# Mixer weights: the lo part made by a ScalarE copy and an adding transfer instead of a VectorE subtraction

## The chip, the cores and the metric

The kernel runs on one core of one Trainium2 chip. The core has five engines that run side by side, each in the order of its own program: TensorE (PE in the views, PEld for its weight loads), VectorE (DVE), ScalarE (ACT), GpSimd (POOL) and SyncE (SP), which here issues the DMA transfers. They wait for one another through semaphores. The metric is device time in microseconds (us), lower is better.

## What is computed

Two transformer networks, one after the other, on one sequence of 512 tokens with 1024 features, all in float32. Cut to its stages:

```python
def first_block(x, ...):
    for layer in range(2):
        h = rmsnorm(x, norm_mix[layer])
        x = x + (even_mixer(h, ...) if layer == 0 else odd_mixer(h, ...))
        x = x + square(relu(rmsnorm(x, norm_mlp[layer]) @ w_up[layer])) @ w_down[layer]
    return rmsnorm(x, norm_final)

def second_block(x, ...):
    h = x + hybrid_mixer(rms_norm(x, attn_norm_g), ...)
    u = rms_norm(h, ffn_norm_g)
    h = h + (silu(u @ w_gate) * (u @ w_up)) @ w_down
    return rms_norm(h, final_norm_g)
```

The even mixer projects to queries, keys and values of two kinds of attention with eight heads each (one with a forget gate, one in chunks with a relative bias) and projects the joined heads back. The odd mixer has stick-breaking attention and an attention with latent queries and keys. The hybrid mixer has differential attention, and attention over compressed, selected and windowed keys, gated and merged. So a mixer is a set of matrix products with weights around many small softmax chains; an MLP is matrix products with weights alone.

## The kernel before, in words

Activations lie with features on the 128 partitions and the 512 tokens along the free side. Every matrix product with weights is made of three passes in a fast reduced float32 form: a value is split into a hi part (rounded to that form) and a lo part (the rest), and the product is hi x hi + hi x lo + lo x hi. Weights are packed in DRAM in blocks of 128 partitions by at most 1120 columns, mostly 1024 (512 KB, eight tiles of 128 x 128). Method `wblock` (L585) fetches and splits one block: SyncE loads it into a buffer `wr` (two of these), ScalarE copies it into `wh`, the hi part, with rounding, and VectorE writes `wl`, the lo part, as `wr - wh`. `wh` and `wl` have two buffers each. `gemm` (L595) and `gemm_iter` then issue for each of the eight tiles two matmuls with `wh` and one with `wl`, 24 of 512 columns for a block; `gemm_tok` (L614) uses the block as the moving side, with the lo part in the second matmul of a group. All matmuls of a group add into one PSUM tile and so keep their order.

All operations are first recorded, with their dependencies, by class `Recorder`; `schedule` then lays them out once, before the launch. It simulates the engines with fixed costs (`cost`, L322) and latencies, gives out buffers in turn, and so fixes the order of each engine's program; a transfer costs its issuer 450 or 625 ns there, and lands 650 ns after the issue and its bytes at 360 per ns, one transfer after another (L477). On the chip that order stays, whatever the real durations. All rows of the trace therefore have one line, L372, that of the issuing helper; operations are told apart by their tiles.

Names that matter beside `wr`, `wh`, `wl`: `h` normalised activations; `psg`, `pss`, `psp`, `pso` PSUM tiles for products, scores, transposes and heads; `AB`, `QS`, `KK` queries and keys, split by ScalarE and VectorE and moved into the heads' layout by SyncE's transfers; `x`, `P` softmax tiles and the residual, parked in DRAM as `xs`; `sm` small columns, sums among them; `acc` sums of squares; `rbcq` and `acc` also hold weights of the compression. In the softmax, VectorE adds the bias and takes the extremum, ScalarE exponentiates, VectorE inverts the sum, GpSimd multiplies by it.

The first two blocks of all, of `fox_v0`, are fetched by `load` between the loads of the eight tiles of x. The names of the weights used below: those that begin with up, down or gate belong to the MLPs, yb and out2 are the last two products of the hybrid mixer, and all others are in the mixers.

Of the kernel before, what the change touches and what calls it, by code (L numbers as in the profile page):

```python
# [11 lines left out]
F32 = mybir.dt.float32  # L12
F32R = mybir.dt.float32r
I32 = mybir.dt.int32
AF = mybir.ActivationFunctionType
ALU = mybir.AluOpType
AX = mybir.AxisListType

T = 512
# [226 lines left out]
def size(ap):  # L246
    return math.prod(n for _, n in ap.ap[1:])


class Recorder:  # L250
# [71 lines left out]
    def cost(self, op):  # L322
        n = max(size(a) for a in op.acc[1] + op.acc[0])
        out = op.args[0]
        psum = any(str(a.space).endswith("PSUM") for a in op.acc[0])
        e = op.eng
        k = sum(isinstance(a, AP) for a in op.args[2:]) + sum(isinstance(a, AP) for a in op.kw.values())
        if op.name == "dma_start":
            return 450 if str(op.args[1].space).endswith("DRAM") else 625
        if e == "tensor":  # L330
            n = size(out)
            if op.name == "transpose":
                return 107
            if op.args[2].dtype == F32:
                return max(4 * n / 2.4, 428)
            return n / 2.4 + 2.5
        if e == "scalar":
            return 93 + 0.833 * n - (40 if psum else 0) + 93 * k
        if e == "vector":
            if op.name == "reciprocal":  # L340
                return 67 + 6.3 * n
            if op.name in ("memset", "tensor_copy") or (op.name == "tensor_scalar" and not psum):
                return 67 + 0.53 * n + 58 * k
            if op.name == "scalar_tensor_tensor":
                return 67 + 1.05 * n + 60 * (k - 1)
            return 67 + 1.05 * n
        if op.name == "tensor_scalar":
            return 160 + 0.836 * n + 83 * k
        if op.name == "affine_select":
            return 90 + 1.2 * n  # L350
        if op.name == "memset":
            return 36 + 0.83 * n
        return 958 if n <= 4 else 60 + 2.3 * n
# [37 lines left out]
    def schedule(self):  # L391
# [25 lines left out]
        dma, last, table = 0.0, None, TABLE[AF.Exp]  # L417
# [4 lines left out]
        while len(order) < len(ops):  # L422
            best = None
            for e in engs:
                if avail[e]:
                    s = clock[e]
                elif pend[e]:
                    s = max(clock[e], pend[e][0][0])
                else:
                    continue  # L430
                if best is None or s < best[0]:
                    best = (s, e)
            if best is None:
                raise RuntimeError("no instruction is ready: " + str({t: len(w) for t, w in waiting.items() if w}))
            now, e = best
            while pend[e] and pend[e][0][0] <= now:
                k = heapq.heappop(pend[e])[1]
                heapq.heappush(avail[e], (ops[k].prio, k))
            op = ops[heapq.heappop(avail[e])[1]]
            need = [t for t in op.tiles if t not in held]  # L440
            short = None
            for t in need:
                tag = self.tag[t]
                if not free[tag] or turn[t] != at[tag]:
                    short = tag
            if short is not None:
                waiting[short].append(op.n)
                continue
            late = max([free[self.tag[t]][0] for t in need], default=0.0)
            if late > now:  # L450
                heapq.heappush(pend[e], (late, op.n))
                continue
            for t in need:
                tag = self.tag[t]
                heapq.heappop(free[tag])
                held.add(t)
                at[tag] += 1
                for k in waiting[tag]:
                    heapq.heappush(pend[ops[k].eng], (now, k))
                waiting[tag] = []  # L460
            cost = op.cost
            if e == "tensor":
                stat = self.region(op.args[1])
                if stat != last:
                    cost = max(cost, 107)
                last = stat
            elif op.name == "activation" and TABLE.get(op.args[2], table) != table:
                table = TABLE[op.args[2]]
                cost += 1280
            end = now + cost  # L470
            clock[e] = end
            lat = self.LAT[e]
            if op.name == "tensor_tensor_reduce":
                lat = dict.fromkeys(lat, 425)
            if op.name == "dma_start":
                nbytes = 4 * math.prod(n for _, n in op.args[0].ap)
                dma = max(dma, end + 650) + nbytes / 360  # L477
                end = dma
            op.end = end
            order.append(op)  # L480
            for k in op.succ:
                o = ops[k]
                o.ready = max(o.ready, end + lat.get(o.eng, 0))
                o.left -= 1
                if not o.left:
                    heapq.heappush(pend[o.eng], (o.ready, o.n))
            for t in op.tiles:
                users[t] -= 1
                done_at[t] = max(done_at.get(t, 0.0), end + 200)
                if not users[t]:  # L490
                    tag = self.tag[t]
                    heapq.heappush(free[tag], done_at[t])
                    for k in waiting[tag]:
                        heapq.heappush(pend[ops[k].eng], (now, k))
                    waiting[tag] = []
# [7 lines left out]
class Net:  # L503
# [36 lines left out]
    def c(self, key):  # L540
        o, n = self.cst_at[key]
        return self.ct[:, o:o + n]

    BUFS = {"x": 8, "T": 3, "G": 3, "P": 3, "wr": 2, "wh": 2, "wl": 2, "V": 8, "o": 6, "KK": 4, "QS": 2, "AB": 2, "h": 8, "X4": 4,
            "sm": 16, "sm32": 3, "rbc": 1, "rbcq": 1, "strip": 2}
    PBUFS = {"g": 3, "s": 2, "p": 2, "o": 1}

    def tl(self, tag, shape, dt=F32):
        self.n += 1
        bufs = self.BUFS.get(tag, 1)  # L550
        return self.rec.own(self.sb.tile(shape, dt, tag=tag, name=f"{tag}_{self.n}", bufs=bufs), tag, bufs)
# [33 lines left out]
    def wblock(self, key, b, tags=("wh", "wl")):  # L585
        nc = self.nc
        off, w = self.pk.index[key][0][b]
        raw = self.tl("wr", [128, WB])[:, :w]
        hi, lo = (self.tl(t, [128, WT if t[0] == "w" else 1024], F32R) for t in tags)
        nc.sync.dma_start(raw, self.ins["w"][off:off + 128 * w].rearrange("(p c) -> p c", p=128))  # L590
        nc.scalar.activation(hi[:, :w], raw, AF.Copy)
        nc.vector.tensor_tensor(lo[:, :w], raw, hi[:, :w].bitcast(F32), ALU.subtract)
        return hi, lo

    def gemm(self, key, mov, evac, tags="gggggggg", cols=slice(0, 512), kept=None):  # L595
# [1152 lines left out]


def build(pk, vec, cst, arrays, stages=None, reorder=True, **tck):  # L1750
    nc = bacc.Bacc("TRN2", target_bir_lowering=False, num_devices=1)
    ins = {k: nc.dram_tensor(f"in_{k}_dram", a.shape, mybir.dt.from_np(a.dtype), kind="ExternalInput").ap()
           for k, a in arrays.items()}
    out = nc.dram_tensor("out_0_dram", (D, T), F32, kind="ExternalOutput").ap()
    with tile.TileContext(nc, **tck) as tc, ExitStack() as ctx:  # L1755
        net = Net(ctx, tc, pk, vec, cst, ins, out)
        net.run(stages)
        net.rec.run(tc, reorder)
    nc.rec = net.rec
    return nc  # L1760
# [7 lines left out]
```

## Time and profile before

| | us |
|---|---|
| median of three runs | 2078.53 (2075.46 to 2080.16) |
| the profiled execution, its own time | 2076.13 |
| its span, from the first to the last instruction | 2074.1 |
| TensorE busy | 2017.1 |
| VectorE busy | 1131.8 |
| ScalarE busy | 895.1 |
| GpSimd busy | 396.5 |

Busy time of an engine is the time in which at least one of its instructions ran; matmuls overlap, so a busy TensorE need not run at its peak. "Idle before" is the time an engine stood still ahead of an instruction, with the engine or transfer whose signal ended it. The stretches used below are the first mixer (0 to 300 us), the first MLP (300 to 600), the second mixer (600 to 925), the second MLP (925 to 1250), and the third mixer (1250 to 1600, its last two products follow); the bounds are rounded.

### The profile page before, as it was taken

The numbers are of one execution on the slowest core, as the hardware profiler recorded it, in microseconds if no ns is written. First come the engines' busy times: TensorE is split into PE (matmuls) and PEld (weight loads), VectorE is DVE, ScalarE is ACT, GpSimd is POOL, SyncE is SP. The second block draws the span as 40 slices with busy tenths as digits, with TensorE's granted clock in tenths as the row PEclk, the third lists the DMA queues.
The fourth block names the chain that finished last, engine by engine and source line by source line (L and its number), as shares of the span: only waits on it lengthen the run. The fifth ranks groups of instructions, "written<-read, shape, count | busy, mean of one in ns | idle before, by whom it ended". The sixth has DMA issues, their size and how long they took to land. (4 is left out here: it accounts for less than half of the span.)

```text
span 2074.1 us, 27228 instructions
## 1 busy us (share of the span) xinstructions
PE 2017.1 (97%) x9958; PEld 1683.7 (81%) x9958; DVE 1131.8 (55%) x2033; ACT 895.1 (43%) x1621; POOL 396.5 (19%) x524
## 2 busy tenths in 40 slices
PE   8999999999999999999999999989999999999998
PEld 7888878888888877778888888867788888888887
DVE  5667853434445576774434344766786644333334
ACT  5556542322335555653323243543685543222224
POOL 2343210000022463220000014211340221011013
PEclk9999999999999999999999999999999999999999
DMA  6445623333344315632333334473213222223232
GB/s 199 129 129 154 198 83 100 94 99 97 97 139 127 102 62 131 180 115 92 102 93 101 94 122 135 122 182 116 71 42 112 92 101 92 101 93 102 91 102 82
DMA packets 80293, 231.98 MB, mean 112 GB/s; under 512 B 11424, under 2 KB 15392, under 8 KB 80160
## 3 DMA queue, kind: packets, MB, share of 16 engines
q1 hardware_dynamic: 80160, 230.25, 36.8%
q8 instruction: 78, 1.28, 0.3%
q14 instruction: 55, 0.45, 0.1%
HBM read 183.04 MB, written 10.49 MB: 93 GB/s over the span
## 5 line engine op out<-in xcount | busy, mean ns | idle before, releaser
L372 PE MATMUL psg<-h,wh 128*128 128x512 f32 x2688 | 848.4, 393 | 0.9 <-ACT h L372 0.6
L372 ACT ACTIVATE wh<-wr 128x1024 fp32r<-128x1024 f32 (+3 forms) x313 | 326.3, 1042 | 846.0 <-PE psg L372 672.9
L372 PEld LDWEIGHTS psg<-h,wh 128*128 128x128 f32 x2688 | 503.3, 189 | 102.0 <-ACT h L372 1.5
L372 PE MATMUL psg<-h,wl 128*128 128x512 f32 x1344 | 528.9, 393 | 1.2 <-DVE wl L372 1.0
L372 DVE TENSOR_TENSOR wl<-wr,wh 128x1024 fp32r<-128x1024 f32 (+3 forms) x313 | 384.7, 1229 | 59.9 <-ACT wh L372 58.7
L372 PEld LDWEIGHTS psg<-h,wl 128*128 128x128 f32 x1344 | 253.6, 189 | 53.9 <-DVE wl L372 3.1
L372 PE MATMUL psg<-KK,wh 128*128 128x512 f32 (+1 forms) x788 | 237.8, 383 | 0.4 <-DVE V L372 0.2
L372 DVE TENSOR_TENSOR x<-psg,x 128x512 f32<-128x512 f32 (+1 forms) x120 | 78.2, 654 | 281.8 <-PE psg L372 281.7
L372 POOL TENSOR_TENSOR acc<-acc,T 128x512 f32<-128x512 f32 (+1 forms) x50 | 72.9, 1457 | 775.7 <-issue 627.3
L372 PE MATMUL psg<-V,wh 128*128 128x512 f32 (+1 forms) x672 | 205.7, 387 | 1.1 <-DVE G L372 1.1
L372 PEld LDWEIGHTS psg<-KK,wh 128*128 128x128 f32 x788 | 146.3, 188 | 29.5 <-ACT o L372 0.6
L372 PE MATMUL psg<-KK,wl 128*128 128x512 f32 (+1 forms) x394 | 150.8, 383 | 0.0
L372 PEld LDWEIGHTS psg<-V,wh 128*128 128x128 f32 x672 | 125.6, 188 | 27.3 <-ACT wh L372 1.2
L372 DVE SCALAR_TENSOR_TENSOR T<-psg,rbc 128x512 f32<-128x512 f32 x64 | 44.2, 691 | 167.2 <-PE psg L372 166.8
L372 ACT ACTIVATE x<-x,sm 128x128 f32<-128x128 f32 (+1 forms) x192 | 106.6, 558 | 54.7 <-DVE sm L372 53.9
L372 PE MATMUL psg<-V,wl 128*128 128x512 f32 (+1 forms) x336 | 129.9, 387 | 0.0
L372 PE MATMUL psg<-o,wh 128*128 128x512 f32 x384 | 126.2, 397 | 0.8 <-ACT wh L372 0.5
L372 PE MATMUL psg<-wh,h 128*128 128x256 f32 (+2 forms) x560 | 114.5, 292 | 6.6 <-ACT wh L372 6.6
L372 PE MATMUL pso<-pt,V 128*128 128x128 f32 (+3 forms) x432 | 108.8, 340 | 3.4 <-ACT pt L372 1.9
L372 POOL TENSOR_SCALAR x<-x,sm 128x128 f32<-128x128 f32 (+1 forms) x112 | 65.9, 594 | 174.6 <-DVE sm L372 122.8
L372 PEld LDWEIGHTS psg<-wh,h 128*128 128x128 f32 x560 | 92.4, 194 | 8.4 <-ACT wh L372 6.6
L372 POOL TENSOR_TENSOR T<-T,rbc 128x512 f32<-128x512 f32 x22 | 39.2, 1782 | 280.5 <-ACT T L372 280.5
(263 smaller groups left out, 2667.6 us busy)
## 6 DMA issues: line engine op xcount, KB each, us to landing
wr<-in_w_dram SPq DMA_DIRECT2D x302, 512.0 KB, 3.5
KK<-AB SPq DMA_DIRECT2D x48, 256.0 KB, 5.4
QS<-AB SPq DMA_DIRECT2D x48, 128.0 KB, 4.0
x<-xs SPq DMA_DIRECT2D x24, 256.0 KB, 3.3
xs<-P SPq DMA_DIRECT2D x16, 256.0 KB, 3.9
xs<-x SPq DMA_DIRECT2D x16, 256.0 KB, 2.0
h<-AB SPq DMA_DIRECT2D x16, 256.0 KB, 4.1
KK<-AB SPq DMA_DIRECT2D x32, 128.0 KB, 2.3
```

The lines of the kernel that those rows point to most:

```text
L372: op.inst = getattr(getattr(nc, op.eng), op.name)(*op.args, **op.kw)
```

## The change

For the weights of the mixers, all but those that begin with up, down, gate, yb or out2, the lo part is made otherwise. ScalarE writes the hi part as before, then, in a second instruction, the negated hi part into the lo buffer. GpSimd then issues a transfer that reads the same block from DRAM once more and adds it to what the lo buffer holds. VectorE has no part in it, and the buffer `wr` is read by ScalarE's first copy alone. `wh` and `wl` get three buffers for all weights. The scratch memory for the descriptors of transfers that GpSimd issues is set to 4096 bytes a partition. The planner counts 860 ns of GpSimd for such an issue and a landing 1500 ns later than for one of SyncE.

```diff
@@ cost
         if op.name == "dma_start":
+            if op.eng == "gpsimd":
+                return 860
             return 450 if str(op.args[1].space).endswith("DRAM") else 625
@@ schedule
                 dma = max(dma, end + 650) + nbytes / 360
-                end = dma
+                end = dma if e == "sync" else dma + 1500
@@ Net
-    BUFS = {"x": 8, "T": 3, "G": 3, "P": 3, "wr": 2, "wh": 2, "wl": 2, "V": 8, "o": 6, "KK": 4, "QS": 2, "AB": 2, "h": 8, "X4": 4,
+    BUFS = {"x": 8, "T": 3, "G": 3, "P": 3, "wr": 2, "wh": 3, "wl": 3, "V": 8, "o": 6, "KK": 4, "QS": 2, "AB": 2, "h": 8, "X4": 4,
@@ wblock
-        nc.sync.dma_start(raw, self.ins["w"][off:off + 128 * w].rearrange("(p c) -> p c", p=128))
-        nc.scalar.activation(hi[:, :w], raw, AF.Copy)
-        nc.vector.tensor_tensor(lo[:, :w], raw, hi[:, :w].bitcast(F32), ALU.subtract)
+        src = self.ins["w"][off:off + 128 * w].rearrange("(p c) -> p c", p=128)
+        nc.sync.dma_start(raw, src)
+        if key.startswith(("up", "down", "gate", "yb", "out2")):
+            nc.scalar.activation(hi[:, :w], raw, AF.Copy)
+            nc.vector.tensor_tensor(lo[:, :w], raw, hi[:, :w].bitcast(F32), ALU.subtract)
+        else:
+            nc.scalar.activation(hi[:, :w], raw, AF.Copy)
+            nc.scalar.activation(lo[:, :w], hi[:, :w].bitcast(F32), AF.Copy, scale=-1.0)
+            nc.gpsimd.dma_start(lo[:, :w], src, accum_op=ALU.add)
@@ build
-    nc = bacc.Bacc("TRN2", target_bir_lowering=False, num_devices=1)
+    nc = bacc.Bacc("TRN2", target_bir_lowering=False, num_devices=1, dynamic_dma_scratch_size=4096)
```

## Rows read from the trace of the kernel before

**Rows 1.** The page, part 1: busy us, share of the span, instructions.
```profile
PE 2017.1 (97%) x9958; PEld 1683.7 (81%) x9958; DVE 1131.8 (55%) x2033; ACT 895.1 (43%) x1621; POOL 396.5 (19%) x524
```

**Rows 2.** Busy us by stretch: length, engines, granted clock, DMA share, GB/s.
```profile
0.00:300.00 300.00, 285.40 (x1576) 243.40 (x1577) 201.28 (x439) 166.43 (x348) 92.70 (x160) 0.99 0.53 151
600.00:925.00 325.00, 305.89 (x1625) 256.84 (x1624) 218.32 (x415) 180.05 (x375) 114.80 (x187) 0.98 0.43 121
1250.00:1600.00 350.00, 337.04 (x1813) 276.39 (x1812) 242.55 (x634) 186.51 (x429) 92.41 (x110) 0.99 0.39 111
300.00:600.00 300.00, 300.00 (x1325) 248.39 (x1325) 125.78 (x141) 94.23 (x117) 5.38 (x3) 1.00 0.33 101
925.00:1250.00 325.00, 325.00 (x1435) 269.11 (x1435) 138.64 (x162) 109.20 (x138) 11.65 (x8) 1.00 0.33 102
```

**Rows 3.** Matmuls by shape (busy us, mean ns): first mixer, second mixer, first MLP.
```profile
L372 PE MATMUL psg<-h,wh 128*128 128x512 f32 x315 | 105.0, 403 | 0.6 <-ACT h L372 0.6
...
L372 PE MATMUL psg<-h,wh 128*128 128x512 f32 x265 | 85.9, 398 | 0.0
...
L372 PE MATMUL psg<-h,wh 128*128 128x512 f32 x422 | 129.9, 389 | 0.0
```

**Rows 4.** TensorE's waits, whole span: waiter, releaser, us in total, times, longest.
```profile
PE psg L372 <- ACT wh L372: 7.1, 2, 6.6
PE psg L372 <- DMA rbcq<-in_w_dram: 5.5, 2, 5.1
...
PE pss L372 <- DMA KK<-AB: 3.2, 3, 1.4
...
PE pss L372 <- POOL P L372: 0.2, 1, 0.2
```

**Rows 5.** The weight block's operations, 0 to 300 us: count, ns min/median/max, starts.
```profile
L372 SPq DMA_DIRECT2D wr<-in_w_dram x41: 327/333/637, 1.7 to 298.8; - x41
L372 ACT ACTIVATE wh<-wr x39: 1039/1062/1082, 5.5 to 296.4; 128x1024 fp32r<-128x1024 f32 x37, 128x1056 fp32r<-128x1056 f32 x2
L372 DVE TENSOR_TENSOR wl<-wr,wh x39: 1203/1225/1723, 6.6 to 297.5; 128x1024 fp32r<-128x1024 f32 x37, 128x1056 fp32r<-128x1056 f32 x2
```

**Rows 6.** Busy us by stretch (columns as in rows 2), slices of 50 us.
```profile
0.00:50.00 50.00, 41.91 (x233) 37.03 (x234) 28.76 (x50) 25.27 (x44) 11.09 (x19) 1.00 0.68 206
...
200.00:250.00 50.00, 47.97 (x248) 39.83 (x248) 37.88 (x95) 28.56 (x66) 13.44 (x21) 1.00 0.80 227
...
850.00:900.00 50.00, 46.69 (x246) 38.65 (x245) 42.24 (x103) 29.62 (x68) 13.53 (x18) 1.00 0.63 192
...
1500.00:1550.00 50.00, 50.00 (x292) 41.89 (x290) 42.14 (x145) 39.70 (x108) 19.96 (x29) 1.00 0.09 33
```

**Rows 7.** SyncE's queue waits, first and second mixer (columns as in rows 4).
```profile
SPq L372 <- DVE wl L372: 87.3, 22, 8.8
...
SPq L372 <- DVE wl L372: 172.2, 35, 27.4
```

**Rows 8.** ScalarE's wait for a hi buffer, first mixer (columns as in rows 4).
```profile
ACT wh L372 <- PE psg L372: 24.3, 12, 3.9
```

**Rows 9.** GpSimd's instructions by shape, whole span (columns as in rows 3).
```profile
L372 POOL TENSOR_TENSOR acc<-acc,T 128x512 f32<-128x512 f32 x38 | 62.5, 1644 | 755.7 <-issue 627.3 <-ACT T L372 128.3
...
L372 POOL TENSOR_TENSOR sm<-sm,cst 128x4 f32<-128x4 f32 x13 | 13.2, 1019 | 53.8 <-DVE sm L372 52.4 <-DMA wr<-in_w_dram 1.4
```

**Rows 10.** Weight transfers: the page's median us to landing, and the tile's extremes.
```profile
wr<-in_w_dram SPq DMA_DIRECT2D x302, 512.0 KB, 3.5
...
DMA to landing us min/median/max: 1.9/3.5/9.7
```

**Rows 11.** The start, in order of time: start us, us, instruction.
```profile
5.49 1.08 ACT L372 ACTIVATE wh<-wr 128x1056 fp32r<-128x1056 f32 x1 [0.32 <-DMA wr<-in_w_dram]
...
6.61 1.26 DVE L372 TENSOR_TENSOR wl<-wr,wh 128x1056 fp32r<-128x1056 f32 x1 [1.17 <-ACT wh L372]
...
7.92 0.28 PEld L372 LDWEIGHTS psg<-wl,h 128*128 128x128 f32 x1 [0.35 <-DVE wl L372]
```

## The prediction

> **What bounds the kernel now.** I read the shares of the whole span first, then the same shares by stage, then who ended TensorE's waits, then the life of one weight block. TensorE is busy for 97% of 2074.1 us [rows 1]. By stage the reader is to see two kinds of stretch [rows 2]. In the two long MLP stretches (300 to 600 and 925 to 1250) TensorE is never idle, and 1325 matmuls in 300 us make 0.226 us each: nothing there can be gained but by fewer matmuls, and the change takes none away. In the three mixers (0 to 300, 600 to 925, 1250 to 1600) it is busy for 285.40, 305.89 and 337.04 us, so idle for 14.6, 19.1 and 13.0, together 46.7 us. On top of that its matmuls are stretched: one of 512 columns has a mean of 403 and 398 ns in the first two mixers and 389 in the MLPs [rows 3]. Some 10 ns on the 5014 matmuls of the three mixers gives an estimate of 50 us of short waits inside busy time. So what a change of the mixers' side work can give back is some 97 us at the very most, and much of that is dependency latency that no spare engine removes.
>
> What ends TensorE's idle time in the mixers [rows 4]: ScalarE with the weights (7.1 us in two waits, one of 6.6 at the start), DMAs (the two largest, rbcq and KK, 8.7 us), and a scatter of small waits on GpSimd and VectorE. The 27 rows of that view add up to about 13 us for DMA, 12 each for GpSimd and VectorE and 10 for ScalarE, all but 2 or 3 us of it in the mixers. No one engine is the bound. VectorE, however, is the fullest helper: 201.28 + 218.32 + 242.55 = 662.2 us of 975 (68%), against 533.0 (55%) for ScalarE and 299.9 (31%) for GpSimd [rows 2].
>
> **Part 1: the subtraction goes from VectorE to a transfer.** The diff spares the keys that start with up, down, gate, yb and out2. Counting blocks of the other keys in the code gives 32 in the even mixer, 37 in the odd one and 42 in the hybrid one: 111. The trace has 39 weight blocks from 0 to 300 us [rows 5]: 32, and seven of the MLP that begins there. About 101 are full blocks and ten are short. VectorE loses 101 x 1.225 us and ten of some 0.5: 129 us, and falls from 662 to 533 us in the mixers (55%). ScalarE gains as many copies of the size of its first (1.062 us [rows 5]): 101 x 1.06 + 5 = 112 us, and rises to 645 (66%). The busiest helper stays as busy as before, under another name; but before, the two peaks coincide with VectorE above ScalarE in most slices (37.88 against 28.56 in 200 to 250, 42.24 against 29.62 in 850 to 900 [rows 6]), so moving five or six blocks evens them out. In 1500 to 1550 (42.14 and 39.70) it only swaps them.
>
> What this gives: idle time that ends at VectorE or GpSimd is about 24 us [rows 4], and part of GpSimd's waits lead back to VectorE's sums. I take some two fifths of that, 10 us, for VectorE's queue getting a fifth shorter, and 8 us of the 50 us of stretch. Bounds: 0 (it is all latency) to 35 us. Against it ScalarE's longer queue, which stands on the same softmax and evacuation chains: its 10 us of idle time, less the 6.6 of the start, and its part of the stretch grow; I take 3 us, bounds 0 to 10.
>
> **Part 2: SyncE and the buffers.** The raw block is now free when ScalarE has read it, not when VectorE has: 1.2 us sooner at least. SyncE's queue stands 87.3 us in the first mixer (22 times) and 172.2 in the second (35) behind just that release [rows 7], and behind it in the queue stand the KK and QS moves that a head's scores wait for. ScalarE stands 24.3 us (12 times) in the first mixer until TensorE frees a hi buffer [rows 8], with exponentials queued behind; a third buffer removes most of it. Most of these waits are of engines with nothing urgent; I take 2 us of gain, bounds 0 to 15. In the MLPs the third buffer gives nothing, since TensorE has no idle time there.
>
> **Part 3: the adding transfer.** Before, no transfer is issued by GpSimd and none adds, so its prices are bounded. The issue: from SyncE's 0.333 us [rows 5] to the 1.64 us of GpSimd's longest frequent instruction [rows 9]; I take 1.0, nearest to its shortest real job (1.019 [rows 9]). 111 of them put 37 to 182, probably 110 us on GpSimd in the mixers (to 42%). GpSimd is in order: an issue that waits for ScalarE's negated part holds up the normalisations of the softmax behind it. I take 2 us, bounds 0 to 12. The landing: a plain block lands after 3.5 us in the median [rows 10] and 9.7 at worst; I take 5 us, as an adding transfer also reads what it adds to, bounds 3.5 to 9.7. A lo part is then ready 1.06 + 1.0 + 5 = 7 us after its hi part, where it was 1.2 us. A dense block is 24 matmuls, 24 x 0.226 = 5.4 us; with two buffers 7 us could not be hidden, with three there are 16.3 us a cycle, less 5.4 of use: 10.9 us for hi (1.06) and lo (7). That fits with 2.8 us to spare in dense stretches, so I cost the delay at nothing there; the cover is the third buffer, and it is gone when the landing exceeds 7.8 us.
>
> The traffic: in the MLP stretch the DMA engines are busy 0.33 at 101 GB/s [rows 2], which makes 0.52 MB worth 1.7 us of all 16. 111 blocks more are 180 us if they cost as a load, 360 if they cost double, on 0.53 x 300 + 0.43 x 325 + 0.39 x 350 = 435 us now. The mean goes from 45% to 63% or 82% of 975 us. In 200 to 250, at 0.80 already [rows 6], six or seven blocks (39 in 300 us [rows 5]) bring it to 1.0 or more: it is full, and the KK and QS moves queue with it. I take 2 us in all, bounds 0 to 25. The Trainium skill (DMA: Bandwidth & Descriptors, Issuing engines are not separate DMA queues) says that transfers of all issuing engines run on the same 16 engines and interleave; by that rule GpSimd's queue is no second road, and the contention is as worked out here. No row of before shows two issuers. The same page (Anatomy of one DMA, SWDGE path) fits 2.0 us and the bytes at 436 GB/s for one transfer issued by GpSimd, which makes an estimate of 3.2 us for 0.52 MB, said of no adding one; the row of a plain block has 3.5. By it the start (below) costs 1 us less and the sum is 11 instead of 10.
>
> **Part 4: the start.** The first lo part is written by VectorE at 6.61 and used at 7.92 [rows 11]. Each group of the first product needs it as its second matmul, so TensorE can do four and then waits. After the change: 6.57 + 1.1 + 1.0 + 5 = 13.7 us, beside eight loads of x. In the old order TensorE was itself waiting for x in this stretch (41.91 us busy of the first 50 [rows 6]), so I count 3 of the 5.8 us; bounds 0 to 8.
>
> **The sum:** - 10 - 8 - 2 + 3 + 2 + 2 + 3 = -10 us. The profiled execution took 2076.13 us (2.0 outside its span), so 2066.1 of its own; it lies 2.4 us below the median of the runs shown, 2078.53, from which the change gives 2068.5.
>
> **Rivals.** (a) The transfers are the new bound: the doubled price of 360 us and a landing of 8 us and more. Then in the slices that are fullest now (200 to 250 at 0.80, 850 to 900 at 0.63 [rows 6], and two like them) each of the some 20 blocks there is late by 1 to 2 us, beyond the third buffer's 10.9 us. For it: DMA is already the largest ender of idle time [rows 4]. Against: elsewhere there is room (0.09 in 1500 to 1550). Price: 20 x 1.5 = 30 us less the gain of 10, so about 2098. It decides from 3 us of DMA time a block on. (b) GpSimd's order: issues and normalisations hold each other up, one delay of about 0.3 us for half the blocks, 17 us: 2085 with the gains. Against: GpSimd is at 31% and its long waits are for work, not for room. (c) All is hidden: the waits are latency, gains and losses stay below 4 us, 2078. For: no engine but TensorE is full. (d) VectorE's relief counts more: a third of the 97 us, 2047. (e) The change doesn't do what it says, as when VectorE keeps the work: excluded by the diff; a planner that puts the transfers late is case (a).
>
> **How the numbers follow.** Forecast 0.46 (2056 to 2074), (c) 0.20, (a) 0.12, (b) 0.15, (d) 0.07. Within 0.2% is within 4.2 us, about what a measurement of this kernel can tell from no change. Faster: 0.46 + 0.07 = 0.53, less 0.02 of the forecast's own upper end: 0.51. Same: 0.20 + 0.02 = 0.22. Slower: 0.27. The range from 2050 to 2092 leaves out most of (a), half of (d) and a little of (b), about 0.18.
>
> **What would show it.** In the mixers: VectorE near 533 us, ScalarE near 645, GpSimd near 400 or as much above 300 as its issues cost; TensorE's idle time below 46.7 us and its 512-column mean below 400 ns; in the MLPs no change. Rows of adding transfers with a landing of about 5 us. Wrong: TensorE waiting for lo parts by DMA for more than 5 us in all, a DMA share of 1 over whole slices with KK and QS landing later than 5 us, the first use of a lo part after 15 us, or GpSimd's issues at well over 1 us.

## The result and the profile after

The changed kernel takes 2177.42 us (median of four runs, 2169.11 to 2183.42) where the kernel before, on the same chips, takes 2076.99 (2075.14 to 2080.16). The ratio is 1.0472, with a 95% interval from 1.0442 to 1.0501: slower by 100 us, where 10 us less was forecast and 2092 was the upper end of the range. The profiled execution took 2176.73 us, 2174.9 of it as its span.

The page, part 1 (busy us, share of the span, instructions), answers to [rows 1]:

```profile
PE 2050.4 (94%) x9958; PEld 1706.9 (78%) x9958; DVE 1013.8 (47%) x1922; ACT 994.0 (46%) x1732; POOL 468.2 (22%) x635
```

TensorE runs the same 9958 matmuls. It now stands idle for 2174.9 - 2050.4 = 124.5 us, before for 57.0. So 67.5 of the 100.8 us that the span has grown by are idle time, and 33.3 are matmuls that took longer. VectorE lost 118 us of work, as intended, and ScalarE gained 99.

The DMA queues of the page (packets, MB, share of 16 engines' span) and its DMA issues (KB, median us from issue to landing), which answer to [rows 10]:

```profile
q1 hardware_dynamic: 80160, 230.25, 34.7%
q0 software_dynamic: 15984, 54.80, 14.4%
...
wr<-in_w_dram SPq DMA_DIRECT2D x302, 512.0 KB, 3.5
wl<-in_w_dram POOLq DMA_DIRECT2D x96, 512.0 KB, 6.9
KK<-AB SPq DMA_DIRECT2D x48, 256.0 KB, 8.1
QS<-AB SPq DMA_DIRECT2D x48, 128.0 KB, 6.7
```

q0 is the queue that GpSimd issues to. It moves 54.80 MB, 104.5 blocks of 0.52 MB, in 14.4% of 2174.9 us, which is 3.0 us of all 16 engines for one; a plain block was worth 1.7 in the prediction's estimate. An adding transfer lands after 6.9 us. And moves that the change doesn't touch land later: KK from 5.4 to 8.1 us, QS from 4.0 to 6.7. Their rows before:

```profile
KK<-AB SPq DMA_DIRECT2D x48, 256.0 KB, 5.4
QS<-AB SPq DMA_DIRECT2D x48, 128.0 KB, 4.0
```

Busy us by stretch, columns as in [rows 2]: the three mixers, then two slices of [rows 6]:

```profile
0.00:300.00 300.00, 261.90 (x1449) 224.78 (x1449) 153.41 (x392) 185.80 (x364) 110.97 (x191) 0.97 0.80 200
600.00:925.00 325.00, 288.88 (x1498) 244.13 (x1496) 152.22 (x314) 183.53 (x364) 124.72 (x208) 0.95 0.64 151
1250.00:1600.00 350.00, 324.99 (x1653) 261.74 (x1651) 179.89 (x486) 186.22 (x371) 105.93 (x120) 0.97 0.62 153
...
200.00:250.00 50.00, 40.84 (x183) 33.17 (x182) 20.19 (x55) 24.50 (x50) 9.98 (x17) 0.91 0.90 223
850.00:900.00 50.00, 36.93 (x189) 29.88 (x189) 26.49 (x82) 27.55 (x72) 13.18 (x21) 0.89 0.73 169
```

In these 975 us TensorE is idle for 38.1 + 36.1 + 25.0 = 99.2 us, before for 46.7, and that with less work in them, because all of it comes later now (1449 matmuls in the first stretch, before 1576). The DMA share rose from 0.53 to 0.80 in the first mixer, and in its slice from 200 to 250 from 0.80 to 0.90.

Who ended TensorE's waits (us in total, times, longest), which answers to [rows 4]:

```profile
PE psg L374 <- DMA wl<-in_w_dram: 39.5, 15, 10.1
PE pss L374 <- DMA KK<-AB: 9.2, 5, 2.5
```

The first row is new: fifteen times TensorE stood before a lo part that had not landed. One of them, in the second mixer, in order of time (start us, us, instruction, idle time ahead of it). First ScalarE's hi part, then GpSimd's issue, then TensorE:

```profile
887.47 1.05 ACT L374 ACTIVATE wh<-wr 128x1024 fp32r<-128x1024 f32 x1
```

```profile
890.28 0.91 POOL L374 DMA_DIRECT2D wl<-in_w_dram  x1 [9.96 <-ACT wl L374]
```

```profile
891.16 0.70 PE L374 MATMUL psg<-KK,wh 128*128 128x512 f32 x2
898.32 0.79 PE L374 MATMUL psg<-o,wl 128*128 128x512 f32 x1 [6.45 <-DMA wl<-in_w_dram]
898.91 1.05 PE L374 MATMUL psg<-o,wh 128*128 128x512 f32 x2
899.76 0.63 PE L374 MATMUL psg<-o,wl 128*128 128x512 f32 x1
```

And the same stretch by busy time (columns as above), before, in and after the wait:

```profile
888.00:891.00 3.00, 3.00 (x15) 2.30 (x13) 2.27 (x5) 2.92 (x5) 0.71 (x1) 1.00 0.19 44
...
894.00:898.00 4.00, 0.00 (x0) 0.00 (x0) 0.00 (x0) 0.00 (x0) 0.15 (x1) 0.75 1.04 264
...
899.00:902.00 3.00, 3.00 (x9) 2.32 (x8) 0.00 (x0) 0.00 (x0) 0.00 (x0) 0.50 1.08 237
```

The hi part is ready at 888.5, the issue starts at 890.28, TensorE runs out of other work at 891.9, and the lo part is there at 898.3: 9.8 us after the hi part, with 3.4 us of cover. The DMA engines are full in that time (1.04 at 264 GB/s). After 6.45 us of idleness TensorE runs at a granted clock of 0.50, the level of 1.2 GHz, and nine matmuls run in 3 us where fifteen did at 1.00. So this wait is paid twice, and it isn't the only one: in this trace 16 waits of more than 2 us stand between 100 and 1700 us, and behind each of them the granted clock is below 1.00 for some microseconds. Over the whole span the mean granted clock is 0.974, before 0.993. With two levels that makes an estimate of 2 x 0.026 x 2174.9 = 113 us at 1.2 GHz against 2 x 0.007 x 2074.1 = 29 before. At half the clock 84 us more can cost up to 42 us, where TensorE is busy in them; the 33.3 us of longer matmuls fit with that, which is no proof that the clock is all of them.

### The profile page after: what moved, and what is told of

It is laid out like the page before. It is cut to its first block, busy times and chain, and to the rows that moved or that the text cites. A ratio compares the mean times of both kernels' runs of the same rounds, so it can differ in the third digit from the quotient of the medians.

```text
span 2174.9 us, 27524 instructions
## 1 busy us (share of the span) xinstructions
PE 2050.4 (94%) x9958; PEld 1706.9 (78%) x9958; DVE 1013.8 (47%) x1922; ACT 994.0 (46%) x1732; POOL 468.2 (22%) x635
## 3 DMA queue, kind: packets, MB, share of 16 engines
q0 software_dynamic: 15984, 54.80, 14.4%
## 5 line engine op out<-in xcount | busy, mean ns | idle before, releaser
L374 PE MATMUL psg<-h,wh 128*128 128x512 f32 x2688 | 857.5, 396 | 2.6 <-DVE x L374 1.8
L374 PEld LDWEIGHTS psg<-h,wh 128*128 128x128 f32 x2688 | 508.9, 190 | 106.1 <-ACT wh L374 2.2
L374 PE MATMUL psg<-h,wl 128*128 128x512 f32 x1344 | 532.2, 396 | 11.5 <-DMA wl<-in_w_dram 11.4
L374 PEld LDWEIGHTS psg<-h,wl 128*128 128x128 f32 x1344 | 256.3, 191 | 66.3 <-DMA wl<-in_w_dram 14.4
L374 DVE TENSOR_TENSOR wl<-wr,wh 128x1024 fp32r<-128x1024 f32 x202 | 250.3, 1239 | 40.3 <-ACT wh L374 39.6
L374 POOL TENSOR_TENSOR acc<-acc,T 128x512 f32<-128x512 f32 (+1 forms) x50 | 67.6, 1351 | 751.9 <-issue 313.9
L374 POOL DMA_DIRECT2D wl<-in_w_dram x111 | 97.9, 883 | 316.6 <-ACT wl L374 292.8
L374 PE MATMUL psg<-wh,h 128*128 128x256 f32 (+2 forms) x560 | 119.2, 298 | 6.7 <-ACT wh L374 6.7
L374 ACT ACTIVATE wl<-wh 128x1024 fp32r<-128x1024 f32 (+5 forms) x111 | 111.2, 1002 | 1.1
```

The costliest lines, as they stand in the source:

```text
L374: op.inst = getattr(getattr(nc, op.eng), op.name)(*op.args, **op.kw)
```

## The experiments

All times are medians, with the kernel before timed beside them (2075.38 to 2080.46 us); "+67 us" is the difference of these two medians. My theory after seeing the traces was that the transfers themselves cost the time. The rivals were the new order that the planner makes from the changed costs, the third buffers, GpSimd's issues, and lo parts that arrive late because the planner counts a landing too short.

**Buffers alone (e1_buffers).** The kernel before, with three buffers and the scratch memory:

```diff
-    BUFS = {... "wh": 2, "wl": 2, ...}
+    BUFS = {... "wh": 3, "wl": 3, ...}
-    nc = bacc.Bacc("TRN2", target_bir_lowering=False, num_devices=1)
+    nc = bacc.Bacc("TRN2", target_bir_lowering=False, num_devices=1, dynamic_dma_scratch_size=4096)
```

> The kernel before with three buffers of hi and lo parts and the smaller scratch, and nothing else of the change (VectorE still subtracts). Theory A (the adding transfers cost the time: their late landing and their traffic) and theory B (the planner's order, laid out with too short a landing, costs it): within 5 us of the kernel before's 2077. Theory D (the third buffer or the scratch size reorders the program badly): over 2120.

2080.24 us, ratio 1.0019 [1.0007, 1.0032]: +3 us. The buffers are worth nothing by themselves, and they aren't the cause of the 100 us.

**Everything but the transfer (e2_noadd).** The changed kernel without the adding transfer, so that its lo parts are minus the hi part and lack the raw weights:

```diff
-            nc.gpsimd.dma_start(lo[:, :w], src, accum_op=ALU.add)
```

> The changed kernel without the adding transfer: ScalarE writes the hi part and its negative, three buffers, VectorE free of 111 subtractions, no issue by GpSimd and no second read of the weights (left out: the raw weight is never added, so the mixers' lo parts are wrong). It is what the change would be with a transfer at no cost. Theory A and B: 2055 to 2075, the gain that was forecast without its costs. Theory C (ScalarE's 112 us more load hurts): over 2110.

2071.98 us, ratio 0.9980 [0.9962, 0.9998]: -5 us. Its three mixers by stretch:

```profile
0.00:300.00 300.00, 285.13 (x1591) 245.16 (x1592) 166.25 (x410) 200.89 (x383) 85.24 (x160) 0.99 0.52 154
600.00:925.00 325.00, 302.57 (x1597) 256.88 (x1596) 176.56 (x374) 205.76 (x406) 105.71 (x187) 0.96 0.43 120
1250.00:1600.00 350.00, 342.23 (x1840) 280.87 (x1839) 201.48 (x598) 226.17 (x471) 88.85 (x112) 0.99 0.38 113
```

VectorE is down to 544 us and ScalarE up to 633, as much as the change can move. TensorE's idle time is 45.1 us, where it was 46.7. This is the whole benefit with a transfer that costs nothing: 5 us. The other 105 us belong to the transfer, what it does, and the order planned with it.

**The transfer alone (e3_spare).** The kernel before, VectorE's subtraction, two buffers and all. Beside it, for each mixer block, ScalarE copies one column of the hi part into a spare tile and GpSimd issues the same adding transfer into that tile, which nobody reads (three such tiles in turn, and a scratch memory of 2048 bytes). The planner counts it as in the change:

```diff
         nc.vector.tensor_tensor(lo[:, :w], raw, hi[:, :w].bitcast(F32), ALU.subtract)
+        if not key.startswith(("up", "down", "gate", "yb", "out2")):
+            src = self.ins["w"][off:off + 128 * w].rearrange("(p c) -> p c", p=128)
+            sp = self.spare[:, self.nsp % 3, :w]
+            self.nsp += 1
+            nc.scalar.activation(sp[:, 0:1], hi[:, 0:1].bitcast(F32), AF.Copy)
+            nc.gpsimd.dma_start(sp, src, accum_op=ALU.add)
```

> The kernel before (VectorE subtracts, two buffers), and for every mixer block a further adding transfer of the same size issued by GpSimd into a spare buffer that nobody reads (three spares; a one-column copy of the hi part by ScalarE ties it to its block). Traffic and issue without the wait for the lo part. If traffic is most of theory A: 2120 to 2150, KK moves landing at about 8 us instead of 5.4, no wait for lo parts. If the late lo parts are most of it: under 2095.

2144.20 us, ratio 1.0327 [1.03, 1.0354]: +67 us, two thirds of the loss, from transfers whose result nobody reads. The only waits on them are ScalarE's, whose copy into a spare tile stood six times, 11.2 us in all, for the transfer that used the tile before. Its queues and landings:

```profile
q0 software_dynamic: 15984, 54.80, 14.4%
...
spare<-in_w_dram POOLq DMA_DIRECT2D x96, 512.0 KB, 7.3
KK<-AB SPq DMA_DIRECT2D x48, 256.0 KB, 8.9
QS<-AB SPq DMA_DIRECT2D x48, 128.0 KB, 6.3
```

KK and QS are as late as in the changed kernel. The work of VectorE and the buffers are those of before, so what is lost here is lost to the issues with their copies, the traffic and the order planned around them. Where TensorE pays for it is only in part to be seen. Its idle time grew by 43.4 us, and KK and QS end 11.9 us of its waits, before 5.1 (3.2 for KK [rows 4], 1.9 for QS); the rest is scattered:

```profile
PE pss L374 <- DMA QS<-AB: 7.4, 2, 5.9
...
PE pss L374 <- DMA KK<-AB: 4.5, 2, 4.2
```

**The old order (e8_oldorder).** The changed kernel's operations, put where the subtraction stood in an order planned with it:

```diff
+        if op.kw.get("split") is not None:
+            lo, raw, hi = op.args[:3]
+            nc.scalar.activation(lo, hi, AF.Copy, scale=-1.0)
+            op.inst = nc.gpsimd.dma_start(lo, op.kw["split"][0], accum_op=ALU.add)
+            return
         op.inst = getattr(getattr(nc, op.eng), op.name)(*op.args, **op.kw)
@@ wblock
-            nc.scalar.activation(lo[:, :w], hi[:, :w].bitcast(F32), AF.Copy, scale=-1.0)
-            nc.gpsimd.dma_start(lo[:, :w], src, accum_op=ALU.add)
+            nc.vector.tensor_tensor(lo[:, :w], raw, hi[:, :w].bitcast(F32), ALU.subtract, split=[src])
```

> The changed kernel's operations in an order laid out as if VectorE still subtracted: the planner sees the subtraction, and where it stood ScalarE's negated copy and GpSimd's adding transfer are issued. Theory B (the order planned with 3.6 us to landing is the loss): faster than the changed kernel, under 2130. Theory A: as slow or slower, 2170 to 2260, as the order now expects a lo part 1.2 us after its hi part and TensorE waits for it block by block.

2199.60 us, ratio 1.0588 [1.057, 1.0606]: +123 us, worse than the changed kernel. That the order was laid out anew isn't the cause; the new one saves 22 us against one that counts on VectorE's subtraction. A better one can still save more, as e4_plan shows below.

**What in the transfer costs: four kernels with one line changed in e3_spare.** Fewer bytes (f1_narrow), the same bytes as plain load from SyncE (f2_syncload), from GpSimd without adding (f3_gpplain), and from ScalarE (g4_actload; there the planner counts no later landing either):

```diff
 e3_spare
-            nc.gpsimd.dma_start(sp, src, accum_op=ALU.add)
 f1_narrow
+            nc.gpsimd.dma_start(sp[:, 0:128], src[:, 0:128], accum_op=ALU.add)
 f2_syncload
+            nc.sync.dma_start(sp, src)
 f3_gpplain
+            nc.gpsimd.dma_start(sp, src)
 g4_actload
+            nc.scalar.dma_start(sp, src)
```

> As e3_spare (the kernel before plus an unread adding transfer per mixer block, which took 2144), but each transfer has 128 columns instead of up to 1120: the same 128 partitions to issue on GpSimd, an eighth of the bytes. If GpSimd's issues (0.88 us each, in order before the softmax normalisations) cause e3's 67 us: over 2125. If the bytes on the 16 DMA engines do: under 2095.

> As e3_spare, but the unread transfer is a plain load of the same block issued by SyncE: the second read of the weights, no adding, nothing on GpSimd. At 1.7 us of DMA time a block instead of the 3.0 of an adding one. If e3's loss goes by DMA time: some 0.57 of 67 us, 2105 to 2120; if it is GpSimd's queue: under 2090; if any second transfer delays SyncE's own queue as much as its bytes' time: over 2130.

> As e3_spare, but the unread transfer issued by GpSimd is plain, not adding: the same bytes from DRAM, the same issue, nothing read back from the buffer. If adding is what costs (the second read of the buffer, 3.0 us of DMA time against 1.7): 2105 to 2120 and a landing near 4.5 us. If the issuing side costs: as e3_spare, 2135 to 2150.

> As f2_syncload (an unread plain load per mixer block on SyncE's queue, 2092), but issued by ScalarE: a second queue that interleaves with SyncE's, descriptors not made by GpSimd. If a second queue beside SyncE's is what makes f3_gpplain (2110) dearer than f2: 2105 to 2120, QS moves landing at 5 us. If it is GpSimd's issuing: 2088 to 2098.

f1_narrow: 2087.89 us, 1.0034 [1.0016, 1.0053], +7. f2_syncload: 2091.97 us, 1.0052 [1.0035, 1.007], +11. f3_gpplain: 2110.35 us, 1.0143 [1.0108, 1.0178], +30. g4_actload: 2107.30 us, 1.0148 [1.0117, 1.018], +32. f2_syncload hit none of its three ranges; the others came as one of theirs. So with the order replanned the issues and copies, with an eighth of the columns, cost 7 us, the rest of the plain bytes 23 more, the adding 37 more. A plain transfer is also cheaper to issue, 0.58 us of GpSimd's time against 0.88 for an adding one (medians in f3_gpplain and e3_spare); but all of f1_narrow's issues, at 0.88 us, cost 7 us together, so that can be no large part of the 37. The queue and landings of f3_gpplain:

```profile
q0 software_dynamic: 15088, 54.80, 8.2%
...
spare<-in_w_dram POOLq DMA_DIRECT2D x96, 512.0 KB, 4.6
KK<-AB SPq DMA_DIRECT2D x48, 256.0 KB, 7.4
QS<-AB SPq DMA_DIRECT2D x48, 128.0 KB, 5.2
```

The same 54.80 MB take 8.2% of 2111.8 us instead of 14.4% of 2140.0, 1.7 us of 16 engines a block instead of 3.0: adding costs 1.8 times a load. And of f2_syncload and g4_actload, one fence each:

```profile
spare<-in_w_dram SPq DMA_DIRECT2D x96, 512.0 KB, 3.9
KK<-AB SPq DMA_DIRECT2D x48, 256.0 KB, 7.5
QS<-AB SPq DMA_DIRECT2D x48, 128.0 KB, 3.9
```

```profile
spare<-in_w_dram ACTq DMA_DIRECT2D x96, 512.0 KB, 4.2
KK<-AB SPq DMA_DIRECT2D x48, 256.0 KB, 6.7
QS<-AB SPq DMA_DIRECT2D x48, 128.0 KB, 5.0
```

With the same plain bytes on SyncE's own queue the kernel loses 11 us and QS still lands after 3.9; on a second queue it loses some 30, whether GpSimd or ScalarE issues. So it is not GpSimd's way of issuing that makes the plain transfer dear. That the transfers of a second queue share the engines with a small urgent move, where on SyncE's queue the planner has put that move ahead of them, is a guess that no run shows, and part of the traces speaks against it: KK lands as late on SyncE's queue (7.5 us) as beside a second one (7.4 and 6.7), and KK and QS end 16.4 us of TensorE's waits in f2_syncload, 11.5 in f3_gpplain and 13.4 in g4_actload. Of the 16.4 us by which f3_gpplain's span is longer than f2_syncload's, 6.0 are idle time and 10.4 are longer matmuls. Why a second queue costs more stays open.

**The same with the order held fast (h2_fixed, h3_fixedplain, h4_fixednarrow).** Each kernel above was planned anew. Here the order of before is kept, instruction for instruction, and the copy and the transfer are put behind each mixer block's subtraction without the planner's knowledge:

```diff
+        side = op.kw.pop("side", None)
         op.inst = getattr(getattr(nc, op.eng), op.name)(*op.args, **op.kw)
+        if side is not None:
+            sp, hi, src = side
+            nc.scalar.activation(sp[:, 0:1], hi, AF.Copy)
 h2_fixed
+            nc.gpsimd.dma_start(sp, src, accum_op=ALU.add)
 h3_fixedplain
+            nc.gpsimd.dma_start(sp, src)
 h4_fixednarrow
+            nc.gpsimd.dma_start(sp[:, 0:128], src[:, 0:128], accum_op=ALU.add)
```

> The kernel before, each engine's program in its old order, with the unread adding transfer and its one-column copy put in behind each mixer block's subtraction, unknown to the planner. Against e3_spare (2144), whose order was laid out anew. If traffic and issue cost as such: 2130 to 2170. If e3's loss came from the new order: under 2100.

> As h2_fixed with plain transfers from GpSimd. If adding costs more than half of the loss in a fixed order too: 25 to 35 us above the kernel before, 2100 to 2115.

> As h2_fixed with transfers of 128 columns: GpSimd's issue alone, in the old order. 2080 to 2092 if the issue is cheap; over 2110 if GpSimd's normalisations queue behind issues that the planner didn't count.

h4_fixednarrow: 2099.38 us, 1.0089 [1.0067, 1.0111], +19. h3_fixedplain: 2126.23 us, 1.0229 [1.0208, 1.025], +46. h2_fixed: 2168.13 us, 1.0432 [1.0412, 1.0452], +88. Only h2_fixed came as expected: h3_fixedplain lies above its range and h4_fixednarrow between its two. The ladder is the one of the replanned kernels, only steeper: 19 for the issues, 27 more for plain bytes, 42 more for adding. TensorE's waits in h2_fixed, then in h3_fixedplain:

```profile
PE pss L373 <- DMA KK<-AB: 22.6, 5, 7.1
PE pss L373 <- DMA QS<-AB: 17.6, 3, 8.7
```

```profile
PE pss L373 <- DMA KK<-AB: 18.0, 6, 6.4
PE pss L373 <- DMA QS<-AB: 7.1, 2, 5.6
```

Before, KK and QS ended 5.1 us of waits. Here they end 40.2 us in h2_fixed, so 35.1 of the 57 us by which TensorE's idle time grew (114.2 of 2162.9, against 57.0), 25.1 in h3_fixedplain, and 8.2 in h4_fixednarrow. In the old order the contention is shown where it bites: the scores of a head wait for its KK and QS, the longer the more the transfers take of the DMA engines. The replanned order of e3_spare hides 21 of the 88 us.

**A longer landing in the plan (e4_plan).** The changed kernel, with the planner counting the landing 2 us later:

```diff
-                end = dma if e == "sync" else dma + 1500
+                end = dma if e == "sync" else dma + 3500
```

> The changed kernel with the planner told a landing later by 3500 ns instead of 1500 for GpSimd's transfers, which is what the profile shows (6.9 us from the issue). If the late lo parts are the part of the loss that the traffic does not explain (100 less 67 us): 2140 to 2165, TensorE's waits for lo parts under 15 us instead of 39.5. If it is inherent in the traffic: no change, 2170 to 2185.

2146.64 us, ratio 1.0311 [1.0275, 1.0347]: +66, so 34 of the 100 us came from lo parts planned too late. TensorE's waits on them fall by 19.0 us, though not below the 15 that were expected, its whole idle time falls by 18.9 and its busy time by 10.9:

```profile
PE psg L374 <- DMA wl<-in_w_dram: 20.5, 12, 6.4
```

**And the transfer's bytes counted twice (h1_plan2).** On top of e4_plan:

```diff
-                dma = max(dma, end + 650) + nbytes / 360
+                dma = max(dma, end + 650) + nbytes / 360 * (1 if e == "sync" else 2)
```

> e4_plan (2147) with the planner also told that an adding transfer takes twice its bytes of DMA time, as the profile shows (3.0 us against 1.7 a block). If the 67 us are an order laid out for too little DMA time: 2100 to 2130. If they are in the transfers' place beside the moves, whatever the order: 2140 to 2155.

2134.05 us, ratio 1.0262 [1.0246, 1.0278]: +54, between the two ranges expected. A planner that knows the adding transfer's real price gets some 12 us more, by two intervals that just touch, and half of the loss stays.

**The start (g1_start).** e4_plan, with the first mixer product's blocks (key fox_v0) subtracted by VectorE:

```diff
-        if key.startswith(("up", "down", "gate", "yb", "out2")):
+        if key.startswith(("up", "down", "gate", "yb", "out2", "fox_v0")):
```

> e4_plan (the changed kernel with the corrected landing, 2147) with the first two blocks of all (fox_v0) made by VectorE's subtraction as before. The changed kernel stands 10.4 us there for the first lo part. If that wait lies on the path that sets the end: 2135 to 2141. If x's loads cover it, as the prediction counted: 2143 to 2149.

2137.65 us, ratio 1.0302 [1.0274, 1.0331], beside 1.0311 for e4_plan: 2 us by the ratio, inside both intervals. The start's wait of 10 us is worth little of it, and how much isn't settled.

**A fourth lo buffer (g2_lo4).** e4_plan, with the weight tiles 1120 columns wide and a smaller scratch memory to make room:

```diff
-WT = 1152
+WT = 1120
-    BUFS = {... "wh": 3, "wl": 3, ...}
+    BUFS = {... "wh": 3, "wl": 4, ...}
-... dynamic_dma_scratch_size=4096)
+... dynamic_dma_scratch_size=2048)
```

> e4_plan with a fourth buffer for lo parts. If lo parts are still late through lack of buffers: 2125 to 2140. If what is left is the transfers' traffic and not the lo parts: 2142 to 2152.

2169.38 us, ratio 1.0442 [1.0408, 1.0476]: +94, worse by 28 us than with three, and outside both ranges expected. The lo parts come little sooner: TensorE's waits on them are 16.7 us, in e4_plan 20.5. Why the kernel is slower is open, and the edit changes three things. TensorE's idle time is 105.6 us in both, so all 24.4 us by which the profiled span is longer are longer matmuls, at a mean granted clock that is no lower (0.982 against 0.980). In the first MLP, where nothing adds, those of `h` with `wh` took 395 ns and those of `KK` with `wh` 394, where e4_plan's took 392 and 389, so some of the loss lies outside the changed stretches.

**Half of the transfers (g3_half).** e3_spare, with every second transfer left away:

```diff
+            if self.nsp % 2:
-            nc.gpsimd.dma_start(sp, src, accum_op=ALU.add)
+                nc.gpsimd.dma_start(sp, src, accum_op=ALU.add)
```

> e3_spare (unread adding transfers beside the kernel before, 2144) with every second of the 111 transfers. If the loss goes with the DMA engines' time: half of 67 us, 2107 to 2118. If it comes from the stretches that are full, where half the transfers leave room: under 2100.

2126.45 us, ratio 1.0242 [1.0218, 1.0267]: +51. Half of the transfers cost three quarters of the 67 us. Neither expectation held. The loss isn't proportional to the bytes, and it doesn't vanish where half of the transfers leave room (mean DMA shares of 0.66, 0.55 and 0.49 in the three mixers); the mechanism behind this stays open.

## Why the prediction was wrong

**The bound, and the 97 us at most.** Right as a bound: no variant's median lies below 2071.98 us. But it was read as room for gains only; the same waits had room to grow, and did.

**Part 1, what VectorE's relief gives (-10 and -8, against it +3).** The loads came as forecast (544 for 533 us, 633 for 645 in e2_noadd). The gain didn't. With part 2 the sum was -17; e2_noadd measures -5. TensorE's idle time in the mixers fell by 1.6 us, not by 10, and its busy time over the whole span by 1.5 us, not by 8. The reason that the prediction named for its lower bound fits: these waits are latency of the chain, and VectorE at 56% instead of 68% ends them no sooner. ScalarE's rise to 65% went with it, and no run parts the two. In the changed kernel the matmuls of 512 columns became slower, 411 and 403 ns in the first two mixers against [rows 3].

**Part 2, SyncE and the buffers (-2).** Wrong in its mechanism, though small. The waits of [rows 7] and [rows 8] went under other names. SyncE's queue in the first and second mixer, then ScalarE in the first:

```profile
SPq L374 <- ACT wh L374: 89.3, 20, 9.6
...
SPq L374 <- ACT wh L374: 100.2, 20, 20.1
```

```profile
ACT wh L374 <- PE psg L374: 27.2, 13, 7.4
```

In the first mixer SyncE stands as long for ScalarE as it did for VectorE (89.3 us for 87.3); in the second it stands 100.2 for 172.2, beside fewer blocks. ScalarE still stands for a hi buffer although there are three. e1_buffers says the same: +3 us.

**Part 3, the issue (1.0 us taken).** Right: 0.88 us in the median (111 of them, 741 to 1176 ns). Issues and copies together, with an eighth of the columns, cost 7 us replanned and 19 in the old order, where the order term was 2, with bounds of 0 to 12.

**Part 3, the landing (5 us taken, bounds 3.5 to 9.7).** 6.9 in the median, from 3.6 to 11.4, the slowest beyond the bound. Here stands the first failed step: the delay of the lo part was costed at nothing, as covered by the third buffer. I set one estimated value against the cover of 7.8 us; the measured median leaves 0.9 us of that, and the slowest landings pass it by 3.6. And the 10.9 us of lead were taken from the number of buffers alone, while the order that the planner lays out decides how much of the lead is used. It counted 1500 ns more than for a load, and in the wait shown above the lead was 3.4 us (888.5 to 891.9) where the lo part needed 9.8. e4_plan, in which only the planner's landing differs, measures what that cost: 34 us. The Trainium skill (DMA: Bandwidth & Descriptors, Anatomy of one DMA, SWDGE path) fits 2.0 us and the bytes at 436 GB/s for one transfer, by which I made an estimate of 3.2 us. This kernel's traces are above it: a plain transfer from GpSimd landed after 4.6 us in the median beside the other traffic, an adding one after 6.9 to 7.5.

**Part 3, the traffic (+2, bounds 0 to 25).** This is the step that failed most. The double price was seen as possible and is nearly so (3.0 us a block, 1.8 times). The sum then asked only in which slices the engines would be full, and costed the rest at nothing. But e3_spare loses 67 us with a mean share of 0.60 to 0.81 in the mixers, and f3_gpplain 30 with 0.49 to 0.68; with the issues taken off, 60 us stand where 2 were taken and 25 was the bound, and 69 in the old order. What the sum left out is shown there: KK and QS, landing after 8.5 and 6.8 us in h2_fixed, end 35.1 us more of TensorE's waits. A share below 1 over 300 us hides that the engines are full for microseconds at a time (1.04 in 894 to 898, when three raw blocks, three lo parts and four moves of AB had been issued since 888.5). That this is all of it is not shown: f2_syncload has shares of 0.51 to 0.66 and loses 11 us, and half of the transfers cost three quarters.

**Part 4, the start (+3).** The lo part was ready at 18.0 us where 13.7 was worked out: the issue came at 8.5 and the landing took some 9 us instead of 5. In order of time, three engines:

```profile
7.16 1.07 ACT L374 ACTIVATE wl<-wh 128x1056 fp32r<-128x1056 f32 x1
```

```profile
8.54 1.05 POOL L374 DMA_DIRECT2D wl<-in_w_dram  x1 [8.03 <-ACT wl L374]
```

```profile
18.02 0.59 PE L374 MATMUL psg<-wl,h 128*128 128x264 f32 x1 [10.09 <-DMA wl<-in_w_dram]
```

Of these 10.09 us g1_start got back some 2, inside the noise, so the term may stand.

**A term that was not in the sum.** The clock. TensorE's granted clock fell to 1.2 GHz in or after waits like the one shown, and 33 of the 101 us are matmuls at that level or stretched otherwise. The split is about the same in the experiments with a large loss: 22.5 of the 65.9 us by which the span grew in e3_spare, 31.6 of 88.8 in h2_fixed. To idle time that these kernels bring, about half as much has to be added. That is no rule: it was a third as much in f2_syncload (5.5 to 15.8), as much again in h4_fixednarrow (12.4 to 12.4), and g2_lo4 has longer matmuls than e4_plan without a lower clock.

**The rivals.** (a) comes nearest: the price of 3.0 us a block is just the point from which it was to decide, and the waits on lo parts are there. But it let them arise from landings of 8 us and more against the lead of 10.9 us, where the median is 6.9 and the lead was shorter, and its 30 us were too few, since they held the late lo parts and neither the late KK and QS nor the clock. (b) named 17 us for GpSimd's issues and what they hold up; f1_narrow has 7 and h4_fixednarrow, in the old order, 19, ScalarE's copies and an eighth of the columns included, so it was there, of that size at most, beside something larger. (c) falls with the result, (d) with e2_noadd: the subtraction's move from VectorE to ScalarE is worth 5 us, not a third of 97. Of the prediction's own signs of being wrong two came plainly, 39.5 us of waits on lo parts and their first use at 18.0 us; one came by half, KK after 8.1 us, at a DMA share of 0.90 and not 1; GpSimd's dear issue did not. The chance of 0.12 for (a) was too low, given that its double price was one of two values between which no row decided.

What makes the sum now, of the 105 us between e2_noadd and the changed kernel: 67 for issues and traffic (7, 23 and 37) and about 34 for lo parts planned too late. That leaves 4 of the 105; the parts come from kernels that differ in their order, so it isn't more than a rough account.

## What to carry to other kernels

Work that is taken off an engine which ends few of the bottleneck's waits gives little; here VectorE's 118 us were worth 5, and the transfers put in their place cost 105. Don't cost a new transfer by the mean DMA share alone; look at what it does to the urgent small moves beside it, and add it alone to the old kernel, in the old order and unread by anyone: that one run told more than the sum. Where a planner sets the order, tell it the landing that the trace shows; its wrong figure alone was worth 34 us.

## What the runs showed of the hardware that was not expected

An adding transfer of 0.52 MB takes 3.0 us of all 16 DMA engines where a plain one takes 1.7, and lands after 6.9 to 7.5 us where a plain one issued by GpSimd lands after 4.6. The same plain bytes cost the kernel 11 us on SyncE's own queue and 30 or 32 on a second one, whether GpSimd or ScalarE issues them, with QS after 3.9 against 5.2 and 5.0 us. The Trainium skill (DMA: Bandwidth & Descriptors, Issuing engines are not separate DMA queues) says that transfers of all these engines run on the same 16 DMA engines and interleave, whichever started them. The trace agrees in that KK lands late with each of the three (7.5, 7.4 and 6.7 us, before 5.4). GpSimd issues an adding transfer in 0.88 us and a plain one in 0.58, SyncE a plain one in 0.33 [rows 5]. After 6.45 us of idle time TensorE's granted clock was 0.50 for the next microseconds, and over the kernel the mean went from 0.993 to 0.974.
